# A fixed TensorE order for sliding-window attention, its two halves side by side

## The chip, the cores and the metric

The kernel runs on one core of a Trainium2 chip. The metric is the device time of one execution in microseconds, lower is better. TensorE multiplies matrices from SBUF into PSUM; VectorE, ScalarE and GpSimd (POOL in the profile) do the elementwise work; SyncE issues most of the weight transfers.

## The reference

Two decoder layers over 16 meta tokens and 256 tokens (272 columns), model width 2048, in float32. Layer 0 is a gated linear attention and an MLP with a squared ReLU of width 8192; the change leaves both alone. Layer 1 is the part that matters:

```
k, v   = split(rmsnorm(h) @ w_kv)          # 4 shared key/value heads of 64, rotary on k
q      = rope(rmsnorm(h) @ w_q) / 8        # 32 query heads of 64, 8 to a key/value head
s      = q k^T  on the 16 meta keys and a window of 128 keys, causal; the head's sink joins the softmax
h      = h + (softmax(s) v) @ w_out
h      = h + relu(rmsnorm(h) @ w_up)^2 @ w_down
out    = rmsnorm(h)[16:]
```

## The kernel before

Activations lie with features on the 128 partitions and tokens along the free axis. Every weight is split on the chip into two parts, `hi` (ScalarE, L85) and `lo` (VectorE, L87), and a product of 256 tokens takes two TensorE records per 128x128 weight block: `hi` times both parts of x (512 columns, L105) and `lo` times the high part (256 columns, L106). `product` (L112) runs the two halves of K of one output tile, each half 8 pairs of such records behind one 512 KB weight block. The `hi` and `lo` tiles have 3 buffers each.

Layer 1's queries are 16 tiles of 128 features. A tile holds two heads of 64: the upper 64 partitions belong to one key/value head of a pair of heads, the lower 64 to the other. The loop at L643 to L654 goes over 2 pairs and 4 steps, each with two query tiles, so 8 steps:

- `queries` (L632): two products, `total` (L122) on ScalarE and VectorE, the scaling at L636, then `rope` (L502): four DMAs on POOL's queue swap the halves of each head (L508) and three VectorE operations follow (L510 to L512). L639 puts the step's last 16 tokens aside.
- `scores` (L561): for tokens 16..143 against 128 keys and for tokens 128..255 against 256 keys, two heads of the upper 64 rows, then two of the lower (L573). These are float32 matmuls, two TensorE records each, over 64 rows. Each half writes its own PSUM bank. `soft` (L539) adds the mask and takes the maximum on VectorE (L542), `normalise` (L545) does the exponentials on ScalarE (L553) and the scaling on VectorE (L559).
- `values` (L580), one step later: 12 transposes (L586), three copies by ScalarE (L588), then the products with V, where one half of the output columns goes to 64 partitions and the other to the other 64 (L595 to L597). L599 and L600 split the result into the operand `O`.
- At a pair's last step, `last_scores` (L602) and `last_values` (L614) handle the last 16 tokens of all 16 heads of the pair.

Then `residual` (L132) adds the output product in two rounds (L665): round one takes the first half of K, which is the first pair's output, for all 16 output tiles, round two the second half.

Scores, transposes and value products share a pool of 4 PSUM banks (`aux`, L70); the weight products have 4 more. No order is written out: the framework's planner, which simulates the engines, picks the order of the instructions on each engine, TensorE too, so the pieces of attention stand where the planner found a place for them, between records of the query products and of round one.

Of the kernel before, what the change touches and what calls it, by code (L numbers as in the profile page):

```python
# [11 lines left out]
F32 = mybir.dt.float32  # L12
# [48 lines left out]
def trunk(ctx: ExitStack, tc: tile.TileContext, a: dict, out: bass.AP):  # L61
# [28 lines left out]
    class Split:  # L90
        """A float32 tile as hi | lo, side by side."""
# [5 lines left out]
    def passes(ps, hi, lo, xs, first, last, m=P):  # L97
        """ps[m] += sum over the tiles of w.T @ x: hi hi + hi lo + lo hi (the small terms beside the large where a bank holds both)."""
# [48 lines left out]
    class Square:  # L147
        """Sum of squares over features, then 1 / rms on every partition."""
# [52 lines left out]
    # ================= layer 0: gated linear attention =================  # L201
# [7 lines left out]
    with ExitStack() as gla:  # L209
# [4 lines left out]
        # low-rank gate input  # L214
# [18 lines left out]
        # log gate and its running sum inside each chunk (times 16)  # L233
# [26 lines left out]
        # token-major values  # L260
# [19 lines left out]
        # scores, [key, query] for each head, two heads at a time: the first 128 tokens, first to last 128, the last 128  # L280
# [3 lines left out]
        def scores(hp):  # L284
# [7 lines left out]
            def head_products(dst, n, lhs, rhs):  # L292
                """dst[g] = lhs.T @ rhs over the two feature tiles of head g."""
# [33 lines left out]
            # decays from and to the chunks' ends  # L327
# [14 lines left out]
            # inside a pair of chunks  # L342
# [6 lines left out]
            # between the pairs: keys reach the pair's end, queries from its start  # L349
# [6 lines left out]
            # from the meta tokens  # L356
# [9 lines left out]
            # among the meta tokens, every level at once  # L366
# [118 lines left out]
    # ================= layer 1: sliding window over shared keys and values =================  # L485
    X = slice(NM, L)
    rs1 = sq1.rstd(D, "rs")
    with ExitStack() as swa:
# [13 lines left out]
        def rope(dst, src, cols):  # L502
            """dst = src * cos + swapped(src) * sin for two tiles, the halves of each head swapped by DMA."""
# [30 lines left out]
        # normalised outputs, split; query tiles over tokens: 16..127 (with 128..143 for fill), 128..255, 256..271  # L534
# [10 lines left out]
        def normalise(prs, mx, sink):  # L545
            """Softmax in place of the masked scores, the sink in the sum."""
# [13 lines left out]

        def scores(pair, j, QR):  # L561
            """Softmax for tokens 16..255 of the heads in query tiles 2 j and 2 j + 1 of the pair."""
            m0 = pair * GRP + 2 * j
            sk = sinks[:, 2 * m0:2 * m0 + 4]
            probs = []
            for o, n, mask in ((0, P, m1), (N1, SEQ, m2)):
                mx = ap.tile([P, 4], F32, tag="mx", bufs=4, name="mx")
                ss = []
                for par in range(2):
                    pp = slice(par * HD, (par + 1) * HD)  # L570
                    s = aux.tile([P, 512], F32, tag="aux", name="s")
                    for i in range(2):
                        nc.tensor.matmul(s[:, i * n:(i + 1) * n], QR[pp, i, o:o + P], KR[pp, pair, :n], start=True, stop=True)  # L573
                        ss.append(s[:, i * n:(i + 1) * n])
# [188 lines left out]
```

## Time and profile before

| | |
|---|---|
| runs of the kernel | 2244.43, 2245.18, 2245.67 us (median 2245.18) |
| profiled execution, first to last instruction | 2243.4 us |
| TensorE busy | 2216.4 us (99%), 15432 records |
| VectorE / ScalarE / GpSimd busy | 1397.3 (62%) / 1030.1 (46%) / 259.4 us (12%) |
| granted TensorE clock, mean of the span | 0.996 |
| moved by DMA | 383.57 MB, 171 GB/s |

The span is the profiled execution's own time; the profile shows nothing around it. A busy share is the share of the span in which an engine had an instruction under way. The ends of TensorE's records are modelled, so the distance between starts says more than the length of a record. A float32 matmul shows as two records. In the rows, L573 is scores, L586 transposes, L595 to L597 values, L625 values of the last 16 tokens, L608 their scores.

### The profile page before, as it was taken

How to read it: one execution, taken by the hardware profiler on the slowest of the kernel's cores; microseconds unless marked ns; L12 is line 12 of the kernel's file. 1: busy time of each engine (PE TensorE's matmuls, PEld its weight loads, DVE VectorE, ACT ScalarE, POOL GpSimd, SP SyncE). 2: the span in 40 equal slices, each digit the busy share in tenths (PEclk: the TensorE clock that was granted, in tenths of full speed). 3: DMA queues.
4: the chain of work that ended last, by engine and by line, in shares of the span. 5: the costliest groups of instructions: out<-in, count | busy, mean ns of one | idle time of the engine just before them, and what ended most of it. 6: DMA issues, size and time to landing. Idle time of an engine off the chain costs nothing. (4 is left out here: it accounts for less than half of the span.)

```text
span 2243.4 us, 37921 instructions
## 1 busy us (share of the span) xinstructions
PE 2216.4 (99%) x15432; PEld 2067.8 (92%) x15432; DVE 1397.3 (62%) x2062; ACT 1030.1 (46%) x1541; POOL 259.4 (12%) x279
## 2 busy tenths in 40 slices
PE   8999999999999999999999999999999999999997
PEld 7998999999999999999999988788888888888886
DVE  7767576665545545544556778786656655655665
ACT  4433355444334434433444556555435534534543
POOL 3123132320000000000013112050000000000022
PEclk9999999999999999999999999999999999999998
DMA  5443344565555555555554554346555555555552
GB/s 199 160 141 104 123 145 157 179 214 172 178 177 173 178 176 174 178 177 173 177 175 155 171 166 142 122 159 228 191 188 188 182 196 188 188 188 188 188 188 94
DMA packets 107007, 383.57 MB, mean 171 GB/s; under 512 B 13056, under 2 KB 14080, under 8 KB 106832
## 3 DMA queue, kind: packets, MB, share of 16 engines
q1 hardware_dynamic: 104672, 378.14, 49.9%
q0 software_dynamic: 1152, 2.38, 0.4%
q8 instruction: 120, 1.97, 0.4%
q10 hardware_dynamic: 1008, 0.63, 0.1%
q14 instruction: 55, 0.45, 0.1%
HBM read 376.63 MB, written 2.10 MB: 169 GB/s over the span
## 5 line engine op out<-in xcount | busy, mean ns | idle before, releaser
L87 DVE TENSOR_TENSOR lo<-raw,hi 128x1024 fp32r<-128x1024 f32 (+1 forms) x713 | 881.1, 1236 | 590.1 <-ACT hi L85 584.4
L85 ACT CAST hi<-raw 128x1024 fp32r<-128x1024 f32 (+1 forms) x713 | 746.4, 1048 | 1062.6 <-PE ps L109 588.3
L110 PE MATMUL ps<-x,lo 128*128 128x272 f32 x1856 | 538.2, 290 | 2.4 <-DVE lo L87 2.4
L108 PE MATMUL ps<-x,hi 128*128 128x272 f32 x1856 | 538.9, 290 | 0.0
L109 PE MATMUL ps<-x,hi 128*128 128x272 f32 x1856 | 536.3, 289 | 0.0
L105 PE MATMUL ps<-x,hi 128*128 128x512 f32 x1280 | 449.1, 394 | 0.0
L106 PE MATMUL ps<-x,lo 128*128 128x256 f32 x1280 | 360.0, 282 | 0.2 <-DVE lo L87 0.2
L105 PE MATMUL ps<-hid,hi 128*128 128x512 f32 x1024 | 358.3, 395 | 0.0
L109 PEld LDWEIGHTS ps<-x,hi 128*128 128x128 f32 x1856 | 354.1, 191 | 0.3
L110 PEld LDWEIGHTS ps<-x,lo 128*128 128x128 f32 x1856 | 350.1, 189 | 4.6 <-DVE lo L87 3.7
L108 PEld LDWEIGHTS ps<-x,hi 128*128 128x128 f32 x1856 | 350.4, 189 | 1.6 <-issue 0.7
L108 PE MATMUL ps<-hid,hi 128*128 128x272 f32 x1024 | 294.7, 288 | 0.0
L110 PE MATMUL ps<-hid,lo 128*128 128x272 f32 x1024 | 293.9, 287 | 0.0
L109 PE MATMUL ps<-hid,hi 128*128 128x272 f32 x1024 | 293.6, 287 | 0.0
L105 PEld LDWEIGHTS ps<-x,hi 128*128 128x128 f32 x1280 | 240.0, 188 | 54.6 <-issue 1.5
L106 PE MATMUL ps<-hid,lo 128*128 128x256 f32 x1024 | 286.6, 281 | 0.0
L106 PEld LDWEIGHTS ps<-x,lo 128*128 128x128 f32 x1280 | 241.4, 189 | 1.9 <-issue 0.8
L105 PEld LDWEIGHTS ps<-hid,hi 128*128 128x128 f32 x1024 | 192.2, 188 | 44.6
L109 PEld LDWEIGHTS ps<-hid,hi 128*128 128x128 f32 x1024 | 193.7, 189 | 0.0
L108 PEld LDWEIGHTS ps<-hid,hi 128*128 128x128 f32 x1024 | 192.6, 188 | 0.0
L106 PEld LDWEIGHTS ps<-hid,lo 128*128 128x128 f32 x1024 | 192.2, 188 | 0.3
L110 PEld LDWEIGHTS ps<-hid,lo 128*128 128x128 f32 x1024 | 192.2, 188 | 0.0
(194 smaller groups left out, 2089.6 us busy)
## 6 DMA issues: line engine op xcount, KB each, us to landing
raw<-in_w_up SPq DMA_DIRECT2D x256, 512.0 KB, 3.3
raw<-in_w_down SPq DMA_DIRECT2D x256, 512.0 KB, 3.3
raw<-in_w_in SPq DMA_DIRECT2D x96, 512.0 KB, 3.3
raw<-in_w_out_a SPq DMA_DIRECT2D x32, 512.0 KB, 3.3
raw<-in_w_q SPq DMA_DIRECT2D x32, 512.0 KB, 3.4
raw<-in_w_out_b SPq DMA_DIRECT2D x32, 512.0 KB, 3.3
raw<-in_w_kv SPq DMA_DIRECT2D x8, 512.0 KB, 3.2
sw<-qt POOLq DMA_DIRECT2D x32, 64.0 KB, 2.8
```

The lines of the kernel that those rows point to most:

```text
L85: nc.scalar.copy(hi, raw)
L87: nc.vector.tensor_sub(lo, raw, hi.bitcast(F32))
L105: nc.tensor.matmul(ps[:, :2 * n], wh, x.both, start=begin, stop=False)
L106: nc.tensor.matmul(ps[:, n:2 * n], wl, x.hi, start=False, stop=end)
L108: nc.tensor.matmul(ps[:, :n], wh, x.hi, start=begin, stop=False)
L109: nc.tensor.matmul(ps[:, :n], wh, x.lo, start=False, stop=False)
L110: nc.tensor.matmul(ps[:, :n], wl, x.hi, start=False, stop=end)
```

## The change

The functions `scores`, `values`, `last_scores`, `last_values` and `queries` become methods of a class `Step`. Three things differ:

- Inside a score, value or last piece the two 64-row (or 64-column) halves alternate, matmul by matmul. Before, one half's matmuls stood behind the other's.
- `product` calls a function behind each half of a query product, and `residual` one behind given tiles of round one. So each step t of the query phase has four slots, one behind each half product: in slot 0 the transposes of step t-4, in slot 2 its values and then the 128-key scores of step t-2, in slot 3 the 256-key scores of step t-2 (with the last 16 tokens' scores where a pair ends). In step 7, slots 1 and 3 also hold the first pair's last transposes and last values. What is left over of steps 4 to 7 goes behind tiles 1 to 15 of round one.
- All of it, with both rounds of the output product, stands under a manual schedule for TensorE: TensorE issues in program order there. The other engines stay with the planner.

Buffers: softmax tiles 9 of 128 and 256 keys (5 before) and 4 of 272 (5), `QR` 4 (3), `mx` 6 (4). The number of matmuls, transfers and elementwise operations does not change. The diff also drops comments and docstrings. Its core:

```diff
-    def product(src, xs, raws=None, halves=(0, 1)):
+    def product(src, xs, raws=None, halves=(0, 1), after=None):
         n = xs[0].n
         ps = acc.tile([P, 512], F32, tag="acc", name="ps")
         for i in halves:
             raw = raws[i] if raws else fetch(src[i])
             hi, lo = split_weight(raw)
             passes(ps, hi, lo, xs[i * HK:(i + 1) * HK], i == halves[0], i == halves[-1])
+            if after:
+                after()
         return [ps[:, t * n:(t + 1) * n] for t in range(2 if 2 * n <= 512 else 1)]
 ...
-    def residual(src_w, ys, cols, finish, rounds=1):
+    def residual(src_w, ys, cols, finish, rounds=1, between=None):
         for r in range(rounds):
             for m in range(KT):
                 for term in product(src_w[m], ys, halves=(0, 1) if rounds == 1 else (r,)):
                     nc.vector.tensor_add(h[m][:, cols], h[m][:, cols], term)
+                if between and r == 0:
+                    for f in between.pop(m, ()):
+                        f()
                 if r == rounds - 1:
                     finish(m)
 ...
         def soft(s, n, mask, sink, mx):
-            pr = ap.tile([P, n], F32, tag=f"pr{n}", bufs=5, name="pr")
+            pr = ap.tile([P, n], F32, tag=f"pr{n}", bufs=9 if n < L else 4, name="pr")
 ...
+        HALVES = [slice(par * HD, (par + 1) * HD) for par in range(2)]
+        class Step:
+            def __init__(self, pair, j, qs):
+                self.pair, self.j, self.qs = pair, j, qs
+                self.m0, self.ends = pair * GRP + 2 * j, j == GRP // 2 - 1
+                self.qt = ap.tile([P, 2, L], F32, tag="qt", bufs=2, name="qt")[:, :, :SEQ]
+                self.probs = []
+            def query(self, i, after):
+                ps = total(product(a["w_q"][self.m0 + i], xq, after=after))
+                nc.vector.scalar_tensor_tensor(self.qt[:, i], ps, HD ** -0.5, rs1[:, X], ALU.mult, ALU.mult)
+                if i == 1:
+                    self.QR = ap.tile([P, 2, SEQ], F32, tag="QR", bufs=4, name="QR")
+                    rope(self.QR, self.qt, X)
+                    nc.gpsimd.tensor_copy(self.qs[:, 2 * self.j * N3:2 * (self.j + 1) * N3].rearrange("p (i q) -> p i q", i=2), self.QR[:, :, N2:])
+            def scores(self, part):
+                o, n, mask = ((0, P, m1), (N1, SEQ, m2))[part]
+                sk = sinks[:, 2 * self.m0:2 * self.m0 + 4]
+                ss = [aux.tile([P, 512], F32, tag="aux", name="s") for _ in HALVES]
+                for i in range(2):
+                    for s, pp in zip(ss, HALVES):
+                        nc.tensor.matmul(s[:, i * n:(i + 1) * n], self.QR[pp, i, o:o + P], KR[pp, self.pair, :n], start=True, stop=True)
+                mx = ap.tile([P, 4], F32, tag="mx", bufs=6, name="mx")
+                prs = [soft(ss[c // 2][:, c % 2 * n:(c % 2 + 1) * n], n, mask, sk[:, c:c + 1], mx[:, c:c + 1]) for c in range(4)]
                 normalise(prs, mx, sk)
+                self.probs.append(prs)
+                if part and self.ends:
+                    self.last_scores()
+            def transposes(self):
+                self.PT = []
+                for prs, b in ((self.probs[0], 0), (self.probs[1], 0), (self.probs[1], 1)):
+                    pt = aux.tile([P, 512], F32, tag="aux", name="pt")
+                    for c in range(4):
+                        nc.tensor.transpose(pt[:, c * P:(c + 1) * P], prs[c][:, b * P:(b + 1) * P], ident)
+                    t = ap.tile([P, 4, P], F32, tag="PT", bufs=4, name="PT")
+                    nc.scalar.copy(t.rearrange("p c q -> p (c q)"), pt)
+                    self.PT.append(t)
+            def values(self):
+                PT, m0 = self.PT, self.m0
+                ps = aux.tile([P, 512], F32, tag="aux", name="ps_pv")
+                pv = ps[:, :2 * N2].rearrange("p (i q) -> p i q", i=2)
+                for t, q, begin, end in ((0, slice(0, N1), True, True), (1, slice(N1, N2), True, False), (2, slice(N1, N2), False, True)):
+                    for par, kv in enumerate(HALVES):
+                        nc.tensor.matmul(pv[kv, :, q], VT[t // 2][:, self.pair, kv], PT[t][:, 2 * par:2 * par + 2, :q.stop - q.start], start=begin, stop=end)
+                oh, ol = O[:, m0:m0 + 2, 0, :N2], O[:, m0:m0 + 2, 1, :N2]
+                nc.scalar.copy(oh, pv)
+                nc.vector.tensor_sub(ol, pv, oh.bitcast(F32))
+            def last_scores(self):
+                self.last, ss = [], [aux.tile([P, 512], F32, tag="aux", name="s3") for _ in HALVES]
+                for s, kv in zip(ss, HALVES):
+                    nc.tensor.matmul(s[:, :L], self.qs[kv], KR[kv, self.pair], start=True, stop=True)
+                for par, s in enumerate(ss):
+                    g = 2 * self.pair + par
+                    mx = ap.tile([P, 4], F32, tag="mx", bufs=6, name="mx")[:, :1]
+                    self.last.append(soft(s[:, :L], L, m3, sinks3[:, g:g + 1], mx))
+                    normalise(self.last[-1:], mx, sinks3[:, g:g + 1])
+            def last_transposes(self):
+                self.PT3 = []
+                for pr in self.last:
+                    pt = aux.tile([P, 512], F32, tag="aux", name="pt3")
+                    t = ap.tile([P, 3, P], F32, tag="PT3", bufs=2, name="PT3")
+                    for b, nb in enumerate((P, P, NM)):
+                        nc.tensor.transpose(pt[:nb, b * P:(b + 1) * P], pr[:, b * P:b * P + nb], ident)
+                    nc.scalar.copy(t[:, :2].rearrange("p b q -> p (b q)"), pt[:, :2 * P])
+                    nc.scalar.copy(t[:NM, 2], pt[:NM, 2 * P:3 * P])
+                    self.PT3.append(t)
+            def last_values(self):
+                ps = aux.tile([P, 512], F32, tag="aux", name="ps_pv3")
                 for b, nb in enumerate((P, P, NM)):
+                    for t, kv in zip(self.PT3, HALVES):
+                        nc.tensor.matmul(ps[kv, :P], VT[b][:nb, self.pair, kv], t[:nb, b], start=(b == 0), stop=(b == 2))
+                ms = slice(self.pair * GRP, (self.pair + 1) * GRP)
+                src = ps[:, :P].rearrange("p (i q) -> p i q", q=N3)
+                oh, ol = O[:, ms, 0, N2:], O[:, ms, 1, N2:]
+                nc.scalar.copy(oh, src)
+                nc.vector.tensor_sub(ol, src, oh.bitcast(F32))
         xs2, sq2 = [], Square(SEQ)
 ...
-        for f in late:
-            f()
-        ys = [Split(O[:, m].rearrange("p a n -> p (a n)"), SEQ) for m in range(KT)]
-        residual(a["w_out_b"], ys, X, to_mlp, rounds=2)
+        with tc.manual_schedule(engines={mybir.EngineType.PE}):
+            steps = []
+            for t in range(2 * GRP // 2):
+                pair, j = divmod(t, GRP // 2)
+                if j == 0:
+                    qs = ap.tile([P, P], F32, tag="qs", bufs=2, name="qs")
+                steps.append(Step(pair, j, qs))
+                old, before = (steps[t - 4] if t >= 4 else None), (steps[t - 2] if t >= 2 else None)
+                slots = [[], [], [], []]
+                if old:
+                    slots[0].append(old.transposes)
+                    slots[2].append(old.values)
+                    if old.ends:
+                        slots[1].append(old.last_transposes)
+                        slots[3].append(old.last_values)
+                if before:
+                    slots[2].append(partial(before.scores, 0))
+                    slots[3].append(partial(before.scores, 1))
+                def after():
+                    for f in slots.pop(0):
+                        f()
+                for i in range(2):
+                    steps[t].query(i, after)
+            a4, a5, a6, a7 = steps[-4:]
+            late = {1: [a4.transposes], 3: [a4.values, partial(a6.scores, 0)], 4: [partial(a6.scores, 1)],
+                    5: [a5.transposes], 6: [partial(a7.scores, 0)], 7: [a5.values, partial(a7.scores, 1)],
+                    9: [a6.transposes], 11: [a6.values], 12: [a7.transposes], 13: [a7.last_transposes], 15: [a7.values, a7.last_values]}
+            ys = [Split(O[:, m].rearrange("p a n -> p (a n)"), SEQ) for m in range(KT)]
+            residual(a["w_out_b"], ys, X, to_mlp, rounds=2, between=late)
     fin = ctx.enter_context(tc.tile_pool(name="fin", bufs=1))
     sqf = Square(SEQ)
```

## Rows read from the trace of the kernel before

**Rows 1.** The page, part 1: busy us (share of the span) and instructions.
```profile
PE 2216.4 (99%) x15432; PEld 2067.8 (92%) x15432; DVE 1397.3 (62%) x2062; ACT 1030.1 (46%) x1541; POOL 259.4 (12%) x279
```

**Rows 2.** Busy by stretch: us, PE PEld DVE ACT POOL (counts), clock, DMA share, GB/s.
```profile
1283.73:1468.50 184.77, 184.73 (x1080) 146.52 (x1079) 146.90 (x428) 103.39 (x259) 21.73 (x40) 1.00 0.45 146
1300.00:1315.00 15.00, 15.00 (x98) 12.94 (x97) 13.94 (x43) 10.00 (x28) 3.25 (x5) 1.00 0.45 146
```

**Rows 3.** Timeline of TensorE, plain query pairs: start us, us, line, tile, count.
```profile
1283.73 0.39 PE L105 MATMUL ps<-x,hi 128*128 128x512 f32 x1
...
1285.47 0.39 PE L105 MATMUL ps<-x,hi 128*128 128x512 f32 x1
...
1300.10 0.39 PE L105 MATMUL ps<-x,hi 128*128 128x512 f32 x1
```

**Rows 4.** Timeline of TensorE, scores of 128 keys, one half.
```profile
1385.83 0.28 PE L106 MATMUL ps<-x,lo 128*128 128x256 f32 x1
1386.03 0.71 PE L573 MATMUL s<-KR,QR 64*128 64x128 f32 x4
...
1387.01 0.28 PE L106 MATMUL ps<-x,lo 128*128 128x256 f32 x1
```

**Rows 5.** Timeline of TensorE, scores of 256 keys, one half.
```profile
1323.67 0.28 PE L106 MATMUL ps<-x,lo 128*128 128x256 f32 x1
1323.88 1.13 PE L573 MATMUL s<-KR,QR 64*128 64x256 f32 x4
...
1325.27 0.28 PE L106 MATMUL ps<-x,lo 128*128 128x256 f32 x1
```

**Rows 6.** Timeline of TensorE, all scores of the first step.
```profile
1300.42 1.68 PE L573 MATMUL s<-KR,QR 64*128 64x128 f32 x16
...
1302.25 0.39 PE L105 MATMUL ps<-x,hi 128*128 128x512 f32 x1
```

**Rows 7.** Timeline of TensorE, four transposes.
```profile
1398.63 0.39 PE L105 MATMUL ps<-O,hi 128*128 128x512 f32 x1
1398.86 0.60 PE L586 MATMUL pt<-ident,pr 128*128 128x128 f32 x4
...
1399.42 0.39 PE L105 MATMUL ps<-O,hi 128*128 128x512 f32 x1
```

**Rows 8.** Timeline of TensorE, values of one step.
```profile
1318.42 0.43 PE L596 MATMUL ps_pv<-PT,VT 128*64 128x256 f32 x1
1318.44 0.59 PE L595 MATMUL ps_pv<-PT,VT 128*64 128x224 f32 x2
1318.69 0.56 PE L596 MATMUL ps_pv<-PT,VT 128*64 128x256 f32 x2
...
1319.82 1.14 PE L573 MATMUL s<-KR,QR 64*128 64x128 f32 x8
```

**Rows 9.** Timeline of TensorE, last values of one half.
```profile
1379.78 0.39 PE L105 MATMUL ps<-x,hi 128*128 128x512 f32 x1
1380.10 1.01 PE L625 MATMUL ps_pv<-PT,VT 128*64 128x128 f32 x6
...
1381.26 0.39 PE L105 MATMUL ps<-x,hi 128*128 128x512 f32 x1
```

**Rows 10.** Timeline at the end of the stage, TensorE and VectorE.
```profile
1467.98 0.59 PE L597 MATMUL ps_pv<-PT,VT 128*64 128x256 f32 x2
...
1469.20 0.66 DVE L600 TENSOR_TENSOR O<-ps_pv,O 128x480 fp32r<-128x480 f32 x1 [2.79 <-ACT O L599]
```

**Rows 11.** Groups by line, VectorE, 1283.7 to 1468.5: count | busy, mean ns | idle.
```profile
L87 DVE TENSOR_TENSOR lo<-raw,hi 128x1024 fp32r<-128x1024 f32 x47 | 57.0, 1221 | 13.7 <-ACT hi L85 13.0
...
L542 DVE CUSTOM_DVE_ANT_0 pr<-s,m,sinks 128x128 f32<-128x128 f32 (+2 forms) x68 | 25.8, 417 | 13.5 <-PE s L573 11.1 <-PE s L608 2.4
...
L559 DVE TENSOR_SCALAR pr<-pr,sm 128x128 f32<-128x128 f32 (+2 forms) x68 | 17.6, 318 | 0.2
...
L137 DVE TENSOR_TENSOR h<-h,ps 128x256 f32<-128x256 f32 x32 | 13.2, 417 | 6.5 <-PE ps L106 6.3
```

More of the change, by code (lines that the diff above doesn't have):

```diff
@@ L559, in normalise @@
                 nc.vector.tensor_scalar_mul(pr, pr, sm[:, i:i + 1])
[L561 to L574, printed above, removed]
-                prs = [soft(ss[c], n, mask, sk[:, c:c + 1], mx[:, c:c + 1]) for c in range(4)]
-                normalise(prs, mx, sk)
-                probs.append(prs)
-            return probs
@@ L580, in values @@
-        def values(pair, j, probs):
-            m0 = pair * GRP + 2 * j
-            PT = []
-            for prs, b in ((probs[0], 0), (probs[1], 0), (probs[1], 1)):
-                pt = aux.tile([P, 512], F32, tag="aux", name="pt")
-                for c in range(4):
-                    nc.tensor.transpose(pt[:, c * P:(c + 1) * P], prs[c][:, b * P:(b + 1) * P], ident)
-                t = ap.tile([P, 4, P], F32, tag="PT", bufs=4, name="PT")
-                nc.scalar.copy(t.rearrange("p c q -> p (c q)"), pt)
-                PT.append(t)
-            ps = aux.tile([P, 512], F32, tag="aux", name="ps_pv")
-            pv = ps[:, :2 * N2].rearrange("p (i q) -> p i q", i=2)
-            for par in range(2):
-                kv, cs = slice(par * HD, (par + 1) * HD), slice(2 * par, 2 * par + 2)
-                va, vb = VT[0][:, pair, kv], VT[1][:, pair, kv]
-                nc.tensor.matmul(pv[kv, :, :N1], va, PT[0][:, cs, :N1], start=True, stop=True)
-                nc.tensor.matmul(pv[kv, :, N1:], va, PT[1][:, cs], start=True, stop=False)
-                nc.tensor.matmul(pv[kv, :, N1:], vb, PT[2][:, cs], start=False, stop=True)
-            oh, ol = O[:, m0:m0 + 2, 0, :N2], O[:, m0:m0 + 2, 1, :N2]
-            nc.scalar.copy(oh, pv)
-            nc.vector.tensor_sub(ol, pv, oh.bitcast(F32))
@@ L602, in last_scores @@
-        def last_scores(pair, qs):
-            prs = []
-            for par in range(2):
-                kv, g = slice(par * HD, (par + 1) * HD), 2 * pair + par
-                s3 = aux.tile([P, 512], F32, tag="aux", name="s3")
-                nc.tensor.matmul(s3[:, :L], qs[kv], KR[kv, pair], start=True, stop=True)
-                mx = ap.tile([P, 4], F32, tag="mx", bufs=4, name="mx")[:, :1]
-                prs.append(soft(s3[:, :L], L, m3, sinks3[:, g:g + 1], mx))
-                normalise(prs[-1:], mx, sinks3[:, g:g + 1])
-            return prs
@@ L614, in last_values @@
-        def last_values(pair, prs):
-            ps = aux.tile([P, 512], F32, tag="aux", name="ps_pv3")
-            for par in range(2):
-                kv = slice(par * HD, (par + 1) * HD)
-                pt = aux.tile([P, 512], F32, tag="aux", name="pt3")
-                PT3 = ap.tile([P, 3, P], F32, tag="PT3", bufs=2, name="PT3")
-                for b, nb in enumerate((P, P, NM)):
-                    nc.tensor.transpose(pt[:nb, b * P:(b + 1) * P], prs[par][:, b * P:b * P + nb], ident)
-                nc.scalar.copy(PT3[:, :2].rearrange("p b q -> p (b q)"), pt[:, :2 * P])
-                nc.scalar.copy(PT3[:NM, 2], pt[:NM, 2 * P:3 * P])
-                for b, nb in enumerate((P, P, NM)):
-                    nc.tensor.matmul(ps[kv, :P], VT[b][:nb, pair, kv], PT3[:nb, b], start=(b == 0), stop=(b == 2))
-            ms = slice(pair * GRP, (pair + 1) * GRP)
-            src = ps[:, :P].rearrange("p (i q) -> p i q", q=N3)
-            oh, ol = O[:, ms, 0, N2:], O[:, ms, 1, N2:]
-            nc.scalar.copy(oh, src)
-            nc.vector.tensor_sub(ol, src, oh.bitcast(F32))
@@ L632, in queries @@
-        def queries(pair, j, qs):
-            qt = ap.tile([P, 2, L], F32, tag="qt", bufs=2, name="qt")[:, :, :SEQ]
-            for i in range(2):
-                ps = total(product(a["w_q"][pair * GRP + 2 * j + i], xq))
-                nc.vector.scalar_tensor_tensor(qt[:, i], ps, HD ** -0.5, rs1[:, X], ALU.mult, ALU.mult)
-            QR = ap.tile([P, 2, SEQ], F32, tag="QR", bufs=3, name="QR")
-            rope(QR, qt, X)
-            nc.gpsimd.tensor_copy(qs[:, 2 * j * N3:2 * (j + 1) * N3].rearrange("p (i q) -> p i q", i=2), QR[:, :, N2:])
-            return QR
@@ L643, in trunk @@
-        late = []
-        for pair in range(2):
-            qs = ap.tile([P, P], F32, tag="qs", bufs=2, name="qs")
-            for j in range(GRP // 2):
-                QR = queries(pair, j, qs)
-                for f in late:
-                    f()
-                late = []
-                if j == GRP // 2 - 1:
-                    prs = last_scores(pair, qs)
-                    late.append(partial(last_values, pair, prs))
-                late.append(partial(values, pair, j, scores(pair, j, QR)))
+        HALVES = [slice(par * HD, (par + 1) * HD) for par in range(2)]
@@ L660, in to_mlp @@
             sq2.add(h[m][:, X])
-        for f in late:
-            f()
-        ys = [Split(O[:, m].rearrange("p a n -> p (a n)"), SEQ) for m in range(KT)]
-        residual(a["w_out_b"], ys, X, to_mlp, rounds=2)
+        with tc.manual_schedule(engines={mybir.EngineType.PE}):
[27 more added lines that the diff above has]
+            residual(a["w_out_b"], ys, X, to_mlp, rounds=2, between=late)
     fin = ctx.enter_context(tc.tile_pool(name="fin", bufs=1))
```

## The prediction

> **What bounds the kernel now.** I read the page first. TensorE is busy for 99% of the span and VectorE for 62% [rows 1]. Next I cut out the stage that the change rewrites, from the first plain query product (1283.73 us) to the first matmul of the second output round (1468.50 us), and asked for its busy times. TensorE is busy 184.73 of 184.77 us at full granted clock, VectorE 146.90, ScalarE 103.39 [rows 2]. TensorE therefore ends last in this stage, and only its own time counts while nothing else becomes late. Third I read its timeline, record by record, for what each kind of work costs it.
>
> A pair of plain records (L105, then L106) repeats every (1300.10 - 1283.73) / 47 = 0.3483 us. The stage holds 16 query tiles of 16 pairs and 16 output half-tiles of 8, so 384 pairs; 27 of them lie before 1283.73 (the third tile begins at 1285.47, 5 pairs later, so 32 - 5), so 357 are left, which make 124.3 us [rows 3]. The other 184.77 - 124.3 = **60.4 us** are attention: 8 steps of scores, transposes and values, and twice the last 16 tokens.
>
> **What a visit costs TensorE.** I price a piece by the distance between equal records on both sides of it, less one pair.
> - Scores of 128 keys, one half (4 records): 1387.01 - 1385.83 - 0.35 = 0.83 us [rows 4].
> - Scores of 256 keys, one half (4 records): 1325.27 - 1323.67 - 0.35 = 1.25 [rows 5].
> - All 16 records of a step, both halves and both sizes, in one visit: 1302.25 - 1300.10 - 0.35 = 1.80 [rows 3, 6]. Two halves of both sizes by separate visits would be 2 x (0.83 + 1.25) = 4.16. So the second half runs beside the first at no cost, and 0.83 + 1.25 - 1.80 = 0.28 is the price of going in and out once. Four records then cost 0.55 and 0.97.
> - Four transposes: 1399.42 - 1398.63 - 0.35 = 0.44, so 0.11 each, and they pay no such entry [rows 7].
> - Values: from 1318.42 to 1319.82, six records of one column half ran with four of the other beside them, 1.40 us; with the rest of an entry I take 1.60 for both halves [rows 8].
> - Last values, six records of one half: 1381.26 - 1379.78 - 0.35 = 1.13 [rows 9].
>
> **The change, part by part.** Arithmetic, transfers, vector and scalar instructions stay the same in number: 64 + 4 score matmuls, 96 + 12 transposes, 48 + 12 value matmuls. What moves is TensorE's order.
>
> *Pieces.* Each score piece now holds both 64-row halves, each value piece both 64-column halves, and nothing splits a value piece. After:
> - transposes 108 x 0.11 = 11.9;
> - scores of 128 keys 8 x 0.83, less 0.28 for each of 5 that stand right behind values: 5.2;
> - scores of 256 keys 8 x 1.25, less 2 x 0.28: 9.4;
> - the last tokens' scores, joined to those, 2 x 0.5 = 1.0;
> - values 8 x 1.60 = 12.8;
> - last values 1.13 and, joined to values, 0.85: 2.0.
>
> The sum is 42.3, so TensorE's own work shrinks by 60.4 - 42.3 = **18 us**. Bounds on it: if an entry is worth nothing, the joins give 2.3 less; if every piece were as dense as [rows 6], about 2 more.
>
> *Does the alternation hold?* The halves are written as two passes of one half, then two of the other. In [rows 8] a record of L595 starts at 1318.44, between the first L596 at 1318.42 and the next at 1318.69: a pass of the other half starts before the second pass of the first. The Trainium skill, page "TensorE: Matmul & The Clock Gate", Part 3 (The mechanism), states the opposite: "MATMULs are pc-monotone in start AND end". The row speaks against it, if the two passes of a float32 matmul are neighbours in the program, which they are by its emission; by the rule each piece would be one record longer, priced among the rivals.
>
> *Fixed order: hand-overs.* Two pieces now have a consumer right behind them. (1) The last values of the second pair, then the first product of round two, whose first matmul reads the last 16 tokens of O. Everything on TensorE is queued behind it. After the last value record (second of the two at 1467.98) VectorE's L600 ended at 1469.86 [rows 10], some 1.7 us on; the last tokens' subtraction comes behind that, about 0.3 more, while TensorE has about 1.1 of last values to do. The wait is 0.9, or 2.1 with one weight split of 1.22 [rows 11] ahead of it on VectorE; I take 1.5. (2) The first pair's last values in step 7, then 1.25 us of scores, then round one: the scores cover most of that; 0 to 1.7, I take 0.5. Together +2 us.
>
> *Fixed order: banks and VectorE.* Scores and values share 4 PSUM banks, and each score bank is freed by two L542 reductions (0.42 us each). VectorE has in this stage 146.9 us; of it 16 output splits (19.5), L137 (13.2) and the softmax of steps 5 to 7 (3/8 of 25.8 + 17.6 = 16.3) fall behind the query phase, so about 98 us stay inside it [rows 2, 11]. TensorE's query phase after the change is 229 pairs (79.8) plus 25 of pieces = 104.8. So VectorE would run at 93% there. The trace shows it at 13.94 of 15 us with TensorE fully busy [rows 2], so it can be done, but for 15 us, and with TensorE free to take other products. Per score or transpose visit in the query phase the wait lies between 0 and one split (1.22); 10 visits are exposed (six second score pieces, four groups of transposes): 0 to 12 us. I take a third, **4 us**, since the row nearest shows no stall at the same load.
>
> *Covered at no cost.* The rotation (four transfers on POOL's queue, three vector operations) has a whole step, over 13 us, before its scores, which now come two steps later. The softmax has one step, about 16 us, before its transposes. Weight transfers: the same bytes in a shorter stage, 146 x 185 / 173 = 156 GB/s, with the DMA engines 45% busy now [rows 2].
>
> **Sum.** The profiled execution has a span of 2243.4 us and gives no other time of its own; the runs' median is 2245.18, 1.8 above it. -18 + 2 + 4 = -12: span 2231.4, run **2233 us**. Without any wait 2227.
>
> **Rivals.**
> - *VectorE becomes the bound of the query phase.* For: 93% there. Against: its work is the same, and it has slack in the two first steps and the output round. If it sustains only 86%, halfway between the 93% above and the stage's present 80% [rows 2], 98 us take 114, 9 more than TensorE's 105: -18 + 2 + 9, so 2238. At 80% nothing would be left of the gain (2246). The Trainium skill, "TensorEngine Tiling (Array Packing)", section PSUM Bottleneck, warns of this: packing speeds TensorE, not the emptying of PSUM. No row before shows it binding.
> - *Strict order of starts.* Each piece is one record longer: 8 x (0.14 + 0.24 + 0.24) = 5 us, so 2238. That is the rule quoted above; [rows 8] speak against it.
> - *The halves don't overlap in this order.* The second half then costs its own records: 8 x (0.55 + 0.97 + 1.2) + 2.4 = 24, so 2257, slower. Against it: [rows 6], 16 records in the time of eight.
> - *The other side: the fixed order makes visits wait.* Where the planner could put a ready product in front of an unready piece, TensorE now stands. There are 28 visits. If each waits for one split that sits ahead of its producer on VectorE (1.22), that is 34 us: -18 + 2 + 34, so 2263. It decides from 16 / 28 = 0.57 us a visit on. For: four PSUM banks, and a slot with values and scores uses three. Against: the producers have a step's time, except the banks.
>
> **How the numbers follow.** Forecast (2226 to 2236) 0.55; VectorE-bound 0.20, of which a quarter lies above 2241; strict order 0.10; no overlap 0.04; waits at each visit 0.11, of which a third within 4.5 us of the present time. The 8-in-10 range goes from 2225 (no wait, pieces a little denser) to 2244 (VectorE at 82%); above it lie no overlap, most of the waits and the end of the VectorE case. A measurement here can tell 0.2%, 4.5 us, from no change. Faster by more than that: 0.55 + 0.15 + 0.10 = 0.80; slower: 0.04 + 0.07 = 0.11; the rest, 0.09, within.
>
> **What would show it.** Right: the stage from the first plain query product to round two is 173 us or less (185 before, less 12); score pieces of 128 keys hold 8 records in about 0.8 us and of 256 keys 8 in about 1.25; each value piece 12 records of which records of the two halves begin within some 20 ns of each other; TensorE idle only ahead of round two and at some score pieces. VectorE-bound would show as idle TensorE ahead of L105 or L106 ended by the lo of L87, and VectorE near full. Bank waits would show as TensorE idle ahead of L573's successor until L542 or its ScalarE copy. Strict order would show starts paired one record late, and pieces of five record times where four are counted. I am wrong if the stage does not shrink, or if the time is lost elsewhere, in layer 0 or the second MLP, which the change leaves alone.

## The result and the profile after

The changed kernel takes 2234.01 us (median of 4 runs, 2233.08 to 2234.59) against 2244.82 (4 runs, 2244.43 to 2245.67): a ratio of 0.995, with an interval of 0.9936 to 0.9964, so about half a per cent faster. Its profiled execution has a span of 2231.3 us; the sum had said 2231.4.

The page, part 1 (busy us, share, instructions), answers [rows 1]. The counts are the same; TensorE lost 17 us of work:

```profile
PE 2199.5 (99%) x15432; PEld 2059.7 (92%) x15432; DVE 1397.0 (63%) x2062; ACT 1030.1 (46%) x1541; POOL 263.1 (12%) x279
```

The stage between the same two marks, and its query phase, with the columns of [rows 2]:

```profile
1282.70:1456.36 173.66, 169.19 (x1080) 140.07 (x1078) 144.99 (x426) 100.97 (x259) 22.23 (x40) 0.99 0.49 152
1283.00:1385.60 102.60, 102.60 (x652) 85.55 (x650) 89.56 (x266) 61.37 (x158) 19.92 (x35) 1.00 0.55 171
```

The stage shrank from 184.77 to 173.66, by 11.1 us. Behind it both kernels need the same 774.9 us (2243.4 - 1468.5; 2231.3 - 1456.36); the changed kernel came to its start 1.0 us earlier, which I don't count as the change's: the code of layer 0 is untouched, and the runs below reach this mark anywhere from 1283.26 to 1285.21. By the stage alone the span would be 2243.4 - 11.1 = 2232.3, so that it met 2231.4 to 0.1 is luck. In the query phase TensorE has no gap at all, and VectorE works 89.56 of 102.60 us. The query and output products again fill 357 pairs, 124.3 us, so attention takes 49.4 us of the stage where it took 60.4. By my count of the timeline, TensorE enters a half-array piece (64 rows or 64 columns) 25 times where it did 49 times; scores right behind values count as an entry of their own.

The pieces on TensorE's timeline (start, us, line, tile, count): scores of 128 keys, then of 256, twelve transposes, values with scores, values alone. They answer [rows 4, 5, 7, 8].

```profile
1303.84 0.28 PE L106 MATMUL ps<-x,lo 128*128 128x256 f32 x1
1304.05 0.71 PE L592 MATMUL s<-KR,QR 64*128 64x128 f32 x8
...
1305.03 0.28 PE L106 MATMUL ps<-x,lo 128*128 128x256 f32 x1
...
1307.47 0.28 PE L106 MATMUL ps<-x,lo 128*128 128x256 f32 x1
1307.67 1.13 PE L592 MATMUL s<-KR,QR 64*128 64x256 f32 x8
...
1309.08 0.28 PE L106 MATMUL ps<-x,lo 128*128 128x256 f32 x1
...
1324.76 0.28 PE L106 MATMUL ps<-x,lo 128*128 128x256 f32 x1
1324.88 1.47 PE L605 MATMUL pt<-ident,pr 128*128 128x128 f32 x12
...
1326.42 0.28 PE L106 MATMUL ps<-x,lo 128*128 128x256 f32 x1
...
1331.63 0.28 PE L106 MATMUL ps<-x,lo 128*128 128x256 f32 x1
1331.84 1.46 PE L616 MATMUL ps_pv<-PT,VT 128*64 128x224 f32 x12
1333.23 0.71 PE L592 MATMUL s<-KR,QR 64*128 64x128 f32 x8
...
1334.21 0.28 PE L106 MATMUL ps<-x,lo 128*128 128x256 f32 x1
...
1438.36 0.28 PE L106 MATMUL ps<-O,lo 128*128 128x256 f32 x1
1438.57 1.46 PE L616 MATMUL ps_pv<-PT,VT 128*64 128x224 f32 x12
...
1440.30 0.28 PE L106 MATMUL ps<-O,lo 128*128 128x256 f32 x1
```

The distance between the L106 on both sides, less one pair, is 0.84, 1.26 and 1.31 us, then 2.23 for values with scores and 1.59 for values alone. Eight score records of both halves now cost what four of one half cost before (0.83, 1.25). The join saves 1.59 + 0.84 - 2.23 = 0.20.

All waits of TensorE in the stage (total us, times, longest):

```profile
PE ps L105 <- DVE O L652: 3.7, 2, 2.8
PE s L625 <- DVE mx L547: 0.8, 1, 0.8
```

The second stands in the visit that ends with the last tokens' scores, in round one:

```profile
1421.30 0.28 PE L106 MATMUL ps<-O,lo 128*128 128x256 f32 x1
...
1425.30 0.72 PE L625 MATMUL s<-KR,qs 64*128 64x272 f32 x2 [0.81 <-DVE mx L547]
...
1426.28 0.28 PE L106 MATMUL ps<-O,lo 128*128 128x256 f32 x1
```

By distance this visit (values, scores and last scores) takes 4.63 us. The run e4 below, where nothing waits, needs 1.59 + 1.72 = 3.31 for the same pieces in two visits. So the wait costs more than the 0.8 that shows as idle; the rest hides in the modelled length of the records and counts with the pieces below.

The largest wait is the hand-over to round one. Around it TensorE, ScalarE and VectorE show (in brackets the idle time before, and its releaser):

```profile
1385.79 1.02 PE L647 MATMUL ps_pv<-PT,VT 128*64 128x128 f32 x12
1386.74 1.13 PE L592 MATMUL s<-KR,QR 64*128 64x256 f32 x8
...
1388.64 0.25 ACT L651 CAST O<-ps_pv 128x128 fp32r<-128x128 f32 x1
...
1390.36 0.28 DVE L652 TENSOR_TENSOR O<-ps_pv,O 128x128 fp32r<-128x128 f32 x1
...
1390.69 0.80 PE L105 MATMUL ps<-O,hi 128*128 128x512 f32 x1 [2.82 <-DVE O L652]
...
1391.50 0.63 PE L105 MATMUL ps<-O,hi 128*128 128x512 f32 x1
...
1392.14 0.63 PE L105 MATMUL ps<-O,hi 128*128 128x512 f32 x1
...
1393.96 0.40 PE L105 MATMUL ps<-O,hi 128*128 128x512 f32 x1
```

The last values (L647) end about 1386.8, and 1.1 us of scores stand behind them. Their copy (L651) runs on ScalarE only at 1388.64, behind a weight cast (L85, from 1385.78) and four exponentials (L558, from 1387.00); their subtraction (L652) on VectorE only at 1390.36, behind one weight split (L87, from 1386.86), four reductions (L547, from 1388.33) and a scaling (L579). TensorE stands 2.82 us. Then pairs repeat every 0.64 us instead of 0.348, and the window row (stretch, its length, busy us by engine, clock) shows why: the granted clock is 0.50, the 1.2 GHz level, for 3.4 us.

```profile
1390.40:1393.80 3.40, 3.10 (x9) 2.67 (x10) 2.68 (x14) 2.17 (x9) 2.10 (x4) 0.50 0.44 117
```

Five pairs from 1390.69 to 1393.96 took 3.27 us instead of 1.74, so the clock cost 1.5 more. The hand-over to round two, which answers [rows 10]:

```profile
1454.55 0.97 PE L647 MATMUL ps_pv<-PT,VT 128*64 128x128 f32 x12
...
1456.03 0.28 DVE L652 TENSOR_TENSOR O<-ps_pv,O 128x128 fp32r<-128x128 f32 x1
...
1456.36 0.50 PE L105 MATMUL ps<-O,hi 128*128 128x512 f32 x1 [0.85 <-DVE O L652]
```

So the losses that show are 2.82 + 1.5 + 0.80 + 0.85 = 6.0 us, and the pieces themselves take at most 49.4 - 6.0 = 43.4.

### The profile page after: what moved, and what is told of

It is laid out like the page before. It is cut to its first block, busy times and chain, and to the rows that moved or that the text cites. A ratio compares the mean times of both kernels' runs of the same rounds, so it can differ in the third digit from the quotient of the medians.

```text
span 2231.3 us, 37915 instructions
## 1 busy us (share of the span) xinstructions
PE 2199.5 (99%) x15432; PEld 2059.7 (92%) x15432; DVE 1397.0 (63%) x2062; ACT 1030.1 (46%) x1541; POOL 263.1 (12%) x279
## 5 line engine op out<-in xcount | busy, mean ns | idle before, releaser
L85 ACT CAST hi<-raw 128x1024 fp32r<-128x1024 f32 (+1 forms) x713 | 747.0, 1048 | 1099.7 <-PE ps L109 586.4
L87 DVE TENSOR_TENSOR lo<-raw,hi 128x1024 fp32r<-128x1024 f32 (+1 forms) x713 | 880.3, 1235 | 589.0 <-ACT hi L85 581.6
L106 PE MATMUL ps<-x,lo 128*128 128x256 f32 x1280 | 359.4, 281 | 0.0
L106 PE MATMUL ps<-hid,lo 128*128 128x256 f32 x1024 | 286.6, 281 | 0.0
L106 PEld LDWEIGHTS ps<-x,lo 128*128 128x128 f32 x1280 | 241.5, 189 | 0.1
L106 PEld LDWEIGHTS ps<-hid,lo 128*128 128x128 f32 x1024 | 192.2, 188 | 0.3
```

Of the source, the lines that this page charges most:

```text
L85: nc.scalar.copy(hi, raw)
L87: nc.vector.tensor_sub(lo, raw, hi.bitcast(F32))
L106: nc.tensor.matmul(ps[:, n:2 * n], wl, x.hi, start=False, stop=end)
```

## The experiments

My theory: TensorE's pieces shrink because both halves share one visit and alternate, and what is lost again is lost at hand-overs, not to VectorE. The rivals: the alternation is worth nothing, or everything; the fixed order does the work; VectorE limits the query phase.

In the runs below "stage" is the distance between the same two marks, in the run's profiled execution, and an entry is counted as above. 124.3 us of it are plain pairs, the rest is attention with its waits.

### Halves one behind the other (e1)

```diff
-                for i in range(2):
-                    for s, pp in zip(ss, HALVES):
+                for s, pp in zip(ss, HALVES):
+                    for i in range(2):
...
-                for t, q, begin, end in (...):
-                    for par, kv in enumerate(HALVES):
+                for par, kv in enumerate(HALVES):
+                    for t, q, begin, end in (...):
```

(and likewise in `last_values`)

> Everything as in the changed kernel (2234.0 us, stage 173.7 us), but inside each score, value and last-value piece all matmuls of one half stand ahead of the other half's. Theory A (a half can start only when the one or two records ahead of it are running or next): a 128-key piece takes six record times instead of four, a 256-key piece six instead of four, a value piece ten instead of six: 8 x (0.22 + 0.43 + 0.86) = 12 us more, 2246. Theory B (TensorE starts a record of the free half whatever earlier records of the busy half wait, several deep): no difference, 2234 +- 1.5, and the halves' first records still begin within 20 ns of each other. Theory C (no overlap at all in this order): 24 us more, 2258. I expect B, since in the kernel before a value record of one half began beside the first of three waiting records of the other.

Measured: 2238.09 us (8 runs, 2237.06 to 2238.88), 0.997 [0.9959, 0.9981]; stage 176.35. I had expected B; it fell between A and B. Less the waits (2.40 + 0.53 + 0.68), the stage is 172.7; that of the changed kernel, less 6.0, is 167.7. The clock did not fall behind the 2.40 us gap, pairs follow at 0.348 us at once:

```profile
1394.85 0.50 PE L105 MATMUL ps<-O,hi 128*128 128x512 f32 x1 [2.40 <-DVE O L652]
...
1395.30 0.39 PE L105 MATMUL ps<-O,hi 128*128 128x512 f32 x1
...
1395.65 0.39 PE L105 MATMUL ps<-O,hi 128*128 128x512 f32 x1
```

So the alternation is worth 5 us of TensorE's work. It isn't worth anything in the scores (four records of one half, then four of the other, still overlap, starts 13 ns apart). It is worth it in the values, where a half has six records. First the values with scores in this kernel:

```profile
1366.72 0.28 PE L106 MATMUL ps<-x,lo 128*128 128x256 f32 x1
1366.93 1.89 PE L616 MATMUL ps_pv<-PT,VT 128*64 128x224 f32 x12
1368.75 0.72 PE L592 MATMUL s<-KR,QR 64*128 64x128 f32 x8
...
1369.74 0.28 PE L106 MATMUL ps<-x,lo 128*128 128x256 f32 x1
```

2.67 us where alternating halves took 2.23; eight such pieces make 3.5 us, the last values most of the rest. Next the value records (in brackets, behind TensorE's busy time, how many of them touch each stretch), the changed kernel first, then this one:

```profile
1331.83:1332.07 0.24, 0.23 (x2) 0.20 (x4) 0.00 (x0) 0.00 (x0) 1.00 0.00 0
1332.07:1332.26 0.19, 0.19 (x4) 0.14 (x2) 0.00 (x0) 0.00 (x0) 1.00 0.00 0
```

```profile
1366.92:1367.17 0.25, 0.24 (x1) 0.19 (x2) 0.00 (x0) 0.00 (x0) 1.00 0.00 0
1367.17:1367.36 0.19, 0.19 (x2) 0.14 (x1) 0.00 (x0) 0.00 (x0) 1.00 0.00 0
1367.36:1367.57 0.21, 0.21 (x3) 0.19 (x3) 0.00 (x0) 0.00 (x0) 1.00 0.00 0
```

Alternating, two records begin at once. One behind the other, a single record runs in the first stretch, and the second half begins only with the third record of the first half (1367.368 against 1367.362), when three of that half's records still lie ahead of it in the program. With four records a half, three lie ahead from the start, which fits that the scores lose nothing.

### The planner's order (e2)

```diff
-        with tc.manual_schedule(engines={mybir.EngineType.PE}):
+        if True:
```

> The changed kernel without the manual schedule: the planner again picks TensorE's order; emission, alternation and buffers stay. Theory A (one visit for both halves, which only the fixed order guarantees, is what pays): the planner splits pieces again, attention costs 50 us or more in place of 43, less the 6 us of waits that the fixed order brings: 2236 to 2242. Theory B (the alternation and the later emission pay, whoever orders): the pieces stay whole, the waits go, 2228 to 2231. I expect A at its lower end, near 2236.

Measured: 2237.32 us (6 runs, 2236.3 to 2238.11), 0.9968 [0.9956, 0.9979]; stage 177.54: as theory A expected. TensorE waits less (0.4 + 0.3 + 0.85) but the planner cuts the pieces again, into 38 entries against 25. So of the 10.8 us the fixed order brings 3.3 (2237.32 - 2234.01).

### The last values one slot earlier (e3)

```diff
-                        slots[1].append(old.last_transposes)
-                        slots[3].append(old.last_values)
+                        slots[0].append(old.last_transposes)
+                        slots[2].append(old.last_values)
```

> In step 7 the first pair's last transposes go from slot 1 to slot 0 and its last values from slot 3 to slot 2, so that a half query product and a score piece lie between them and round one. Theory A (the 3.2 us gap ahead of round one is the wait for the last tokens' subtraction on VectorE, and the half clock of the 3.4 us behind it comes from the gap): both go, 2.9 + 1.5 = 4.4 us less, 2229.6, granted clock 1.00 in that stretch. Theory B (the clock falls there for another reason): 2.9 less, 2231, with the half clock still there. Theory C (VectorE is late there anyway, round one's operands or weights are next): the wait moves and under 1 us is gained.

Measured: 2230.67 us (4 runs, 2229.58 to 2231.25), 0.9937 [0.9922, 0.9952]; stage 169.34, 4.3 less than the changed kernel: the 2.82 us gap and the 1.5 us behind it. By its time alone the run lies between theories A and B: it gained only 3.3 us, and its profiled execution came to the stage 1.9 us later than the changed kernel's (1284.58 against 1282.70). The clock decides for A. Around round one's start (1389.68) TensorE is full and the granted clock 1.00:

```profile
1386.00:1393.00 7.00, 7.00 (x43) 5.75 (x42) 5.04 (x26) 3.27 (x12) 0.00 (x0) 1.00 0.22 75
```

### All three waits out (e4)

e3's edit, and step 5's values and step 7's last pieces moved in round one:

```diff
-                    5: [a5.transposes], 6: [partial(a7.scores, 0)], 7: [a5.values, partial(a7.scores, 1)],
-                    9: [a6.transposes], 11: [a6.values], 12: [a7.transposes], 13: [a7.last_transposes], 15: [a7.values, a7.last_values]}
+                    5: [a5.transposes], 6: [partial(a7.scores, 0)], 7: [partial(a7.scores, 1)], 8: [a5.values],
+                    9: [a6.transposes], 11: [a6.values, a7.transposes, a7.last_transposes], 14: [a7.last_values, a7.values]}
```

> As the run with the last values early, and two more waits taken out: the values of step 5 go behind tile 8 instead of ahead of step 7's second scores (so the four banks suffice for these and the last tokens' scores), and the last pair's transposes go behind tile 11, its last values and values behind tile 14 instead of 15, so that one more product of round one covers the subtractions. Theory A (the three waits are what is left of the cost of the fixed order): 4.4 + 1.0 + 0.9 less, and 0.3 more for one more entry: 2228. Theory B (the waits come back elsewhere, since VectorE is the bound behind them): 2230 or more.

Measured: 2228.01 us (4 runs, 2227.7 to 2228.95), 0.9927 [0.9912, 0.9941]; theory A. The stage, whole:

```profile
1283.91:1451.19 167.28, 167.28 (x1080) 138.63 (x1079) 142.37 (x423) 99.96 (x258) 23.15 (x40) 1.00 0.47 158
```

TensorE has no gap in it, so 167.3 - 124.3 = 43.0 us is what the pieces cost by themselves; the prediction had 42.3.

### Only the alternation, in the kernel before (e5)

```diff
-                for par in range(2):
-                    pp = slice(par * HD, (par + 1) * HD)
-                    ...
-                    for i in range(2):
+                tiles = [aux.tile([P, 512], F32, tag="aux", name="s") for _ in range(2)]
+                for i in range(2):
+                    for par in range(2):
...
-            for par in range(2):
-                ...
+            for t, q, begin, end in (...):
+                for par in range(2):
```

> The kernel before (2244.9 us, 60.7 us of attention on TensorE, 49 entries into a half mode), with the alternation alone: score and value matmuls are emitted half by half in turn, and the planner orders as before. Theory A (the alternation itself pays little, since TensorE starts the free half's record past three waiting ones anyway, and the planner goes on splitting pieces): 0 to 3 us less, 2242 to 2245, still 40 entries or more. Theory B (the halves' order in the program is what left them unpaired before): 8 us less or more, 2237.

Measured: 2240.49 us (10 runs, 2239.71 to 2241.94), 0.9977 [0.9968, 0.9986]. It is 4.7 us faster than the kernel before on the same chip (2245.21), between the two theories. The stage fell by 6.4 to 178.37, but the planner pushed four value records into round two, that round has two waits (0.4 and 0.2), and it took 1.9 us longer (46.10 against 44.16). 45 entries are left in the stage. So the alternation is worth 4 to 5 us in either order (e1 against the changed kernel: 4.1). With e2 the whole gain comes apart, in this order of steps: the alternation alone brings 4.7 us (e5), with the new places of the pieces in the program and the larger buffers it is 7.6 (e2 against its 2244.89 before), and with the fixed order 10.8. What the buffers bring by themselves was not run.

### Scores joined (e6) and five banks for them (e8)

e6 is e4 with the two score pieces of a step in one visit, where the step doesn't end a pair; e8 is e6 with two more edits:

```diff
-                    slots[2].append(partial(before.scores, 0))
+                    slots[2 if before.ends else 3].append(partial(before.scores, 0))
...
-                        slots[0].append(old.last_transposes)
+                        slots[1].append(old.last_transposes)
...
-    acc = ctx.enter_context(tc.tile_pool(name="acc", bufs=4, space=PSUM))
-    aux = ctx.enter_context(tc.tile_pool(name="aux", bufs=4, space=PSUM))
+    acc = ctx.enter_context(tc.tile_pool(name="acc", bufs=3, space=PSUM))
+    aux = ctx.enter_context(tc.tile_pool(name="aux", bufs=5, space=PSUM))
```

> The kernel with the three waits taken out (2228.0 us), and the 128-key scores of the steps that don't end a pair move from behind the values to the visit of the 256-key scores. Values alone cost 1.59, 128-key scores alone 0.84, both in one visit 2.23, so a change of mode inside a visit still costs 0.20 less than a new one; scores of both sizes in one visit cost 1.80 or less, against 0.84 + 1.26. Theory A (entries are what is left to save): 0.4 each for steps 0 and 1, 0.2 each for 2, 4, 5 and 6, 1.6 us less: 2226.4. Theory B (two score visits' four banks are not free in time, so the transposes or the second scores wait for L547): the gain is lost, 2228 to 2231, with gaps on TensorE that L547's maximum ends.

Measured, e6: 2229.07 us (5 runs, 2228.89 to 2229.88), 0.9927 [0.9915, 0.994]; stage 168.58, 1.3 more than e4, with 18 entries for 24: theory B, though ScalarE's copy ends the longest wait and not the maximum of L547. A joined visit costs 1.70 us where two cost 2.10, but it wants all four banks at once. One joined visit is stretched (2.52 us by distance), and the last transposes wait for ScalarE to empty a bank:

```profile
1337.37 2.39 PE L592 MATMUL s<-KR,QR 64*128 64x128 f32 x16
...
1376.27 0.49 PE L638 MATMUL pt<-ident,pr 128*128 128x128 f32 x3
1378.32 0.55 PE L638 MATMUL pt<-ident,pr 128*128 128x128 f32 x3 [1.56 <-ACT PT L607]
```

> The kernel with joined scores (2229.1 us; 18 entries, 44.5 us of attention with some 2.6 us of waits in it, 1.56 of them ahead of the first pair's last transposes), with the last transposes back in slot 1 and five PSUM banks for attention in place of four, three in place of four for the weight products. Theory A (banks alone made it wait): the waits go, 2.6 less, 2226.5. Theory B (the copies and reductions that empty the banks are late, because ScalarE and VectorE have other work ahead of them): a fifth bank only shifts the wait, 2228 or more. Theory C (three banks are too few for the weight products): TensorE stands ahead of L105 in layer 0 too and the run is 2240 or more.

Measured, e8: 2226.95 us (5 runs, 2226.64 to 2228.55), 0.9923 [0.991, 0.9937]; theory A by its time. The stage:

```profile
1283.26:1449.95 166.69, 166.38 (x1081) 138.49 (x1079) 141.53 (x423) 99.19 (x258) 21.56 (x40) 1.00 0.50 159
```

It is 0.6 us shorter than in e4, so joining pays here. Both waits of e6 are gone: the visit that was stretched costs 1.71, as the others. Which edit did what was not taken apart: the last transposes don't wait in the changed kernel either, where they stand in the same slot with four banks. Three banks for the weight products cost nothing that shows. One visit still waits, that of the first pair's last scores: 2.84 us by distance where e4 has 1.72, of which 0.31 shows as idle. This is the fastest version, 17.9 us faster than the kernel before.

### A load on VectorE (e7, e9)

Both add to e4 subtractions whose result nobody reads. In e7 they need nothing of the phase, in e9 they read the step's scaled queries:

```diff
+                for _ in range(3):
+                    nc.vector.tensor_sub(load1, load1, load1)
                 if i == 1:
```

```diff
+                for _ in range(4):
+                    nc.vector.tensor_sub(load1, self.qt[:, i], self.qt[:, i])
                 if i == 1:
```

> The kernel with the three waits taken out (2228.0 us), with six more VectorE subtractions of 128x384 in each step, whose result nobody reads: 48 of some 0.5 us, about 25 us. VectorE is busy 90.1 of the 105.0 us of the query phase. Theory A (TensorE bounds the phase, VectorE has 15 us free that it can use): the phase grows by about 10 us, to 115, and the run is 2238. Theory B (VectorE's free time can't be used, since it waits in order for ScalarE and the banks): 20 us or more, 2248. Theory C (the subtractions find room in the output round): under 5 us.

Measured, e7: 2231.64 us (2 runs, 2231.55 and 2231.72), 0.9938 [0.992, 0.9956]. It doesn't decide: the planner moved the subtractions, which wait for nothing, ahead, and only 29 of the 48 (16.1 of 26.7 us) fell between 1283 and 1390 us, with one gap of TensorE of 1.1 us. e9 ties them to the phase.

> The kernel with the three waits taken out (2228.0 us, query phase 105.0 us, VectorE busy 90.1 of it), with four VectorE subtractions of 128x256 behind each of the 16 scalings of a query tile, which they read, so that they can't run earlier: 64 of 0.42 us, about 26 us. Theory A (VectorE's free 15 us can be used almost whole): 90 + 26 = 116 us of VectorE work, so the phase grows by 11 us or a little more, 2239 to 2243. Theory B (the free time is lost in waits for ScalarE and for the banks): 20 us or more, 2248. Theory C (the planner puts most of them into the output round): under 5 us, 2233.

Measured, e9: 2231.83 us (2 runs, 2231.82 and 2231.85), 0.9943 [0.9925, 0.9961]. 55 of the 64 subtractions fell into the query phase. The phase in e4, then in this run:

```profile
1283.91:1389.00 105.09, 105.09 (x675) 87.17 (x673) 90.13 (x268) 63.81 (x170) 20.83 (x35) 1.00 0.51 168
```

```profile
1284.59:1392.72 108.13, 107.10 (x675) 87.24 (x673) 106.03 (x320) 63.40 (x162) 18.76 (x35) 1.00 0.50 162
```

The 55 records sum to 23.0 us, but most still run when the next record on VectorE begins, so such a record fills some 0.33 us and not its length of 0.42:

```profile
1323.54 0.42 DVE L583 TENSOR_TENSOR load<-qt 128x256 f32<-128x256 f32 x1
1323.87 0.17 DVE L562 RECIPROCAL sm<-sm 128x4 f32<-128x4 f32 x1
```

VectorE's busy time in the phase rose by 15.9 us and the phase by 3.0, so VectorE is busy 98% of it, and 2.1 of its 15.0 free us are left. By its time the run is nearest to theory C, but C's mechanism is out, since most of the load stayed in the phase. What happened is theory A's mechanism: the free time can be used almost whole, with a load that I had counted too large (26 us). TensorE has 1.0 us of gaps, at transposes that wait for VectorE (`mx` 0.7 us, `pr` 0.3), where e4 has none, and some groups of twelve transposes are stretched from 1.31 to 2.0 and more. The stage took 170.33 us, 3.0 more than in e4, the run 3.8 more. In the changed kernel, at 87%, VectorE is not the bound.

## Why the prediction was right

The forecast (2233, inside 2226 to 2236) came true by its mechanism, but two of its smaller terms were wrong, and that their errors cancel is luck. Two of its own signs failed with them: the stage is 173.66 us, not 173 or less, and TensorE's longest idle time stands ahead of round one, which the signs don't name.

| step of the sum | forecast | shown |
|---|---|---|
| pieces | -18 (42.3 left) | -17.0 to -17.4 (43.4 by the changed kernel less its waits; 43.0 in e4) |
| hand-over to round one | +0.5, at most 1.7 | +4.3 (2.82 idle, 1.5 at half clock) |
| hand-over to round two | +1.5 | +0.85 |
| banks and VectorE in the query phase | +4 (0 to 12) | 0 |
| bank ahead of the last tokens' scores | not priced | +0.8 idle (the rest counts with the pieces) |
| sum | -12 | -11.1 |

**Pieces.** The prices held: 0.84 and 1.26 for scores of both halves (forecast 0.83 and 1.25), 1.59 for values (1.60), 0.109 for a transpose (0.11). Too large was the worth of a join: 0.20 instead of 0.28. I had taken 0.28 from two score sizes in one visit [rows 6]; values followed by scores save less. Two joined score sizes in e6 save 0.40.

**Alternation.** The halves' records start 7 ns apart where a strict order of starts would have set them a record apart; the rival of strict order (2238) is out. The Trainium skill, page "TensorE: Matmul & The Clock Gate", Part 3 (The mechanism), says that starts follow the program's order. e1 shows otherwise: there the second half's first record starts ahead of three records that stand before it in the program. What e1 adds is a limit: written one half behind the other, the second half is held back when six records stand ahead of it and not when four do. No overlap at all (2257) is out too.

**Hand-over to round one.** This is the step that was mis-sized. I let 1.25 us of scores cover most of the copy and the subtraction, and priced the rest at 0 to 1.7 us. The queue ahead of them was longer on both engines: a weight cast and exponentials on ScalarE, then a split, four reductions and a scaling on VectorE, 3.6 us from the last value record to L652. That the clock would fall behind such a gap was not in the sum either. e3 took the gap away and got back 4.3 us of the stage.

**Banks and VectorE.** I charged 4 us for a VectorE at 93%, 98 us of work in the query phase. It had 89.56 and stood at 87%, and TensorE had no gap there. e9 pushed it to 98%, and the stage lost 3.0 us. The rival of VectorE as the bound (2238, at a sustained 86%) is out. The Trainium skill, page "TensorEngine Tiling (Array Packing)", section PSUM Bottleneck, warns that packing leaves the emptying of PSUM where it was. Here that shows as single waits for a bank (e6, 1.56 us; the last tokens' scores, 0.8), not as a VectorE that is full.

**Fixed order.** The rival at 2263 decided from 0.57 us of waiting a visit on; three waits in the 28 visits that it counted came to 4.5 us, 0.16 each, and e2 shows that the planner's order, with fewer waits but more entries, is 3.3 us slower.

## What to carry to other kernels

Price small 64-row or 64-column pieces by the distance between the plain products around them, put both halves into one visit, and alternate them: with six records a half that was worth 5 us here, with four nothing (five was not run). Where the order is fixed by hand, look at what is queued on the other engines between a piece and its consumer, not at the length of that work: moving the last transposes one slot and the last values one slot earlier gave back 4.3 us of the stage here, 3.3 of the run. When pieces are joined further, count the PSUM banks that the joined visit holds: joining lost 1.3 us of the stage with four banks and gained 0.6 with five and one piece moved.

## What the runs showed of the hardware

- Records of the two halves overlap out of program order only so far: two halves of four records overlapped fully (starts 13 ns apart), of two halves of six the second began two records late. Other lengths were not run.
- Going from plain products to one half-array piece and back costs the same whether eight records or four are in it (0.84 against 0.83); going from values to scores without plain products between saves 0.20 us, joining scores of both sizes 0.40 (1.70 against 2.10).
- Around the end of a 2.82 us gap of TensorE the granted clock was at the 1.2 GHz level for 3.4 us; behind a 2.40 us gap in e1 at the same place it was not (pairs at 0.348 us at once). What decides between them was not tried.
- VectorE was 98% busy over 108.1 us while the stage around it lost 3.0 us. Its records overlap: one of 0.42 us filled 0.33.
